# Shared transposes of q and k, a negated maximum, a spare buffer for the solve, and a longer search for the order

## The chip, the cores and the metric

The kernel runs on one core of one Trainium2 chip. The time is device microseconds (us) of one execution; several runs are taken and the median is the figure. A lower time is better.

## The reference

One layer of an encoder with two head groups, on x of 2048 rows and 1024 columns. After an RMSNorm, one projection gives the inputs of both groups:

- the delta-rule group: 4 heads of width 128, a centred convolution of 5 taps and SiLU on q, k and v, then a gated delta rule that is scanned forward and backward, a gated RMSNorm and a SiLU gate;
- the attention group: 8 query heads and 2 key heads of width 64, blocks of 128 queries that see three blocks of keys.

```
q = rotary(rms_norm(q, q_norm_w), cos, sin)
k = rotary(rms_norm(k, k_norm_w), cos, sin)
scores = einsum('bnqhgd,bnkhd->bnhgqk', qb, kb) * (SWA_HEAD_DIM ** -0.5)
scores = where(valid, scores, -inf)
mx = maximum(max(scores, axis=-1, keepdims=True), sink)
p = exp(scores - mx)
denom = sum(p, axis=-1, keepdims=True) + exp(sink - mx)
out = einsum('bnhgqk,bnkhd->bnqhgd', p / denom, vb)
...
m = where(strict, einsum('bhncd,bhnsd->bhncs', k_beta, k) * decay, 0.0)
t_inv = triangular_solve(eye + m, eye, left_side=True, lower=True, unit_diagonal=True)
...
x = x + concatenate([dn, sw]) @ w_out
```

## The kernel before

Matrix products of the projections keep two float32r halves of each operand, a rounded value (`hi`) and the rest (`lo`), and add three products.

**First part** (`phase_a`). `seq_chunk` projects 16 chunks of 128 rows to the attention's q, k and v and stores them in HBM; `gate_pairs` (tiles `pf_z`) and `conv_pair` (tiles `pf_c`, DVE line 241) project the gates and the convolution's inputs. For every chunk, `kv_chunk` and `q_chunk` load their rows and call `rope`: GpSimd (POOL) multiplies with the rotary table (lines 276 to 279), ScalarE (ACT) squares (281), VectorE (DVE) sums (282), POOL takes the power (283, 284), and DVE scales the rows (285). Then the result is split into hi and lo in SBUF (lines 303 and 304 for k, 321 and 322 for q). Each pair of hi and lo is transposed by TensorE (PE) as one 128x128 block: four transposes for a chunk of k (308), four for each of a chunk's two groups of q (326). One ACT copy takes them from PSUM (309, 327). `attend` computes the scores of a chunk in two groups of four heads (343, 344), adds the mask and takes the maximum with the sink as its start (345, DVE), negates the maximum (349), exponentiates (350, ACT), forms the denominator (353 to 357), scales p on POOL (359), transposes p (364), splits it (368, 369) and multiplies with v (371, 372).

**Second part** (`phase_b`). For each of the four delta heads in turn: `pre_front` (transposes, products `gh` at 695, DVE line 704, and line 709, which stores the matrices `m_d` to HBM), `solve`, `invert`, `scan`. `solve` inverts the diagonal 32x32 blocks of all chunks at once: two loads (732 into X, 733 into L), a transposing copy X to L (735), two fills of X on POOL (736, 737), then 31 steps of two DVE instructions (742, 746), and a store (747). `invert` loads these blocks (758), transposes them on DVE (759), puts them into the diagonals of `e1`, `e2` and `e3` by 12 POOL copies (764, 766, 768) for each of four groups `hi`, and multiplies (773, tiles `pi`). `scan` walks 16 steps forward and backward. While head h is scanned, the front, solve and inversion of head h+1 and the output projection of the attention rows (`sw_units`, tiles `pcs`) stand between its steps. The end is the output projection of the delta rows (`out_half`, tiles `pcd`).

**The order.** `set_order` fixes one instruction queue per engine before the program is built. It models the duration of each instruction, plans the whole program backward and forward 12 times, and keeps the plan with the earliest modelled end. The list `started` holds pairs of instructions whose starts must keep the program's order without the second waiting for the first's end.

Of the kernel before, what the change touches and what calls it, by code (L numbers as in the profile page):

```python
# [7 lines left out]
F32 = mybir.dt.float32  # L8
F32R = mybir.dt.float32r
# [6 lines left out]
P = 128  # L16
# [51 lines left out]
def phase_a(ctx, wide, tc, t, ident, nw, bd, gp, mix_sw, kq_d, v_d, zdn_d, zsw_d, q_pool):  # L68
# [24 lines left out]
    for a, src in ((qw, t["qw"]), (kw, t["kw"])):  # L93
        dma(a[:, 0], src.partition_broadcast(P))
        dma(a[:, 1, 0:32], src[32:64].partition_broadcast(P))
        dma(a[:, 1, 32:64], src[0:32].partition_broadcast(P))
    sink = const("sink", [P, NQ], t["sinks"].partition_broadcast(P))
    edge = const("edge", [P, 12, 4])
    half_neg = const("half_neg", [P, 16])
    V.memset(half_neg, -0.5)  # L100
    A.activation(cw, cw, AF.Copy, scale=0.5)
    A.activation(qw, qw, AF.Copy, scale=0.125)

    xhi, xlo = {}, {}

# [166 lines left out]
    def rope(src, n, tab, name):  # L272
        sv = src.rearrange("p (h d) -> p h d", d=64)
        t1 = sp.tile([P, 8, 64], F32, tag="t1", name=f"t1{name}")[:, :n]
        t2 = sp.tile([P, 8, 64], F32, tag="t2", name=f"t2{name}")[:, :n]
        G.tensor_tensor(t1, sv, tab[:, 0:1].to_broadcast([P, n, 64]), ALU.mult)
# [7 lines left out]
        G.tensor_tensor(rs, rs, half_neg[:, :n], ALU.pow)  # L284
        V.tensor_tensor(t1, t1, rs.unsqueeze(2).to_broadcast([P, n, 64]), ALU.mult)
        return t1

    def kv_chunk(c):
        sl = c % 4 + 2
        if c and c % 4 == 0:  # L290
            V.tensor_copy(k2[:, :, :, 0 : 2 * P], k2[:, :, :, 4 * P : 6 * P].bitcast(F32))
            V.tensor_copy(v2[:, 0:2], v2[:, 4:6].bitcast(F32))
        kv = sp.tile([P, 2 * P], F32, tag="kv", name=f"kv{c}")
        dma(kv, kv_d[c])
        kk = kv[:, 0:P]
        vv = kv[:, P : 2 * P].rearrange("p (h d) -> p h d", d=64)
        A.activation(v2[:, sl, :, 0:64], vv, AF.Copy)
        G.tensor_tensor(v2[:, sl, :, 64:128], vv, v2[:, sl, :, 0:64].bitcast(F32), ALU.subtract)
        kn = rope(kk, 2, rope_tab(c, kw, "k"), f"k{c}")
        kd = sp.tile([P, 512], F32R, tag="qd", name=f"kd{c}")  # L300
        kd = kd.rearrange("p (g s a d) -> p g s a d", g=2, s=2, a=2)
        knb = kn.unsqueeze(2).to_broadcast([P, 2, 2, 64])
        A.activation(kd[:, :, 0], knb, AF.Copy)
        V.tensor_tensor(kd[:, :, 1], knb, kd[:, :, 0].bitcast(F32), ALU.subtract)
        pt = pst.tile([P, 4, P], F32, tag="pst", name=f"ptk{c}")
        for g in range(2):
            for s in range(2):
                T.transpose(pt[:, 2 * g + s], kd[:, g, s].rearrange("p a d -> p (a d)").bitcast(F32), ident)
        A.activation(k2[:, :, :, sl * P : (sl + 1) * P], pt.rearrange("p (g s) n -> p g s n", g=2), AF.Copy)

    def q_chunk(c):
        qq = sp.tile([P, 512], F32, tag="qq", name=f"ql{c}")
        dma(qq, q_d[c])
        tab = rope_tab(c, qw, "q")
        r = []
        qa = rope(qq, 8, tab, f"q{c}")
        for g in range(2):
            qn = qa[:, 4 * g : 4 * g + 4]
            qd = sp.tile([P, 512], F32R, tag="qd", name=f"qd{c}_{g}")
            qd = qd.rearrange("p (h a d) -> p h a d", h=4, a=2)  # L320
            A.activation(qd[:, :, 0], qn, AF.Copy)
            V.tensor_tensor(qd[:, :, 1], qn, qd[:, :, 0].bitcast(F32), ALU.subtract)
            q2 = sp.tile([P, 4, P], F32R, tag="q2", name=f"q2_{c}_{g}", bufs=4)
            pt = pst.tile([P, 4, P], F32, tag="pst", name=f"ptq{c}_{g}")
            for j in range(4):
                T.transpose(pt[:, j], qd[:, j].rearrange("p a d -> p (a d)").bitcast(F32), ident)
            A.activation(q2, pt, AF.Copy)
            r.append(q2)
        return r

    def attend(c, q2):
# [3 lines left out]
        k0 = (sl - 1 + lo) * P  # L335
        for g in range(2):
            pr = [sp.tile([P, 3 * P], F32, tag="pr", name=f"pr{c}_{g}_{j}", bufs=6) for j in range(4)]
            st = sp.tile([P, 4, 4], F32, tag="st", name=f"st{c}_{g}")
            mx, nm, den, es = (st[:, i] for i in range(4))
            for j in range(4):  # L340
                hh = 4 * g + j
                ps = pss.tile([P, 3 * P], F32, tag="pss", name=f"s{c}_{hh}")
                T.matmul(ps[:, :n], q2[g][:, j], k2[:, g, 0, k0 : k0 + n], start=True, stop=False)
                T.matmul(ps[:, :n], q2[g][:, j], k2[:, g, 1, k0 : k0 + n], start=False, stop=True)
                V.tensor_tensor_reduce(  # L345
                    pr[j][:, :n], ps[:, :n], mask[:, lo * P : hi * P], 1.0, sink[:, hh : hh + 1],
                    ALU.add, ALU.max, accum_out=mx[:, j : j + 1],
                )
                V.tensor_scalar(nm[:, j : j + 1], mx[:, j : j + 1], -1.0, None, ALU.mult)  # L349
                A.activation(  # L350
                    pr[j][:, :n], pr[j][:, :n], AF.Exp, bias=nm[:, j : j + 1], accum_out=den[:, j : j + 1]
                )
            V.tensor_tensor(es, sink[:, 4 * g : 4 * g + 4], mx, ALU.subtract)
            A.activation(es, es, AF.Exp)
            V.scalar_tensor_tensor(den, den, 1.0, es, ALU.mult, ALU.add)
            V.tensor_scalar(den, den, 2.0, None, ALU.mult)
            V.reciprocal(den, den)  # L357
            for j in range(4):
                G.tensor_scalar(pr[j][:, :n], pr[j][:, :n], den[:, j : j + 1], 1.0, ALU.mult, ALU.mult)  # L359
# [161 lines left out]
def phase_b(ctx, wide, late, tc, t, ident, consts, hp, mix_dn, mix_sw, kq_d, v_d, zdn_d, zsw_d, dp, out):  # L521
# [204 lines left out]
    def solve(h, H):  # L726
        m_d, x_d, _ = H["solve"]
        L = qa.tile([P, 32, 32], F32, tag="L", name=f"L{h}")
        X = qa.tile([P, 32, 32], F32, tag="X", name=f"X{h}")
        lv = [m_d[d].rearrange("u (p y) -> (u p) y", p=4)[:, : 32 * P] for d in range(2)]  # L730
        lv = [a.rearrange("q (r x) -> q r x", x=P)[:, :, :32] for a in lv]
        dma(X[0:64], lv[0])
        dma(L[64:128], lv[1])
        x = X.rearrange("p r c -> p (r c)")
        V.tensor_copy(L[0:64], X[0:64].rearrange("p r c -> p c r"))
        G.memset(x, 0.0)
        G.memset(x[:, ::33], 1.0)
        for c in range(31):
            n = 31 - c
            tm = qa.tile([P, 256], F32, tag="tm", name=f"tm{h}_{c}")  # L740
            tv = tm[:, : n * (c + 1)].rearrange("p (r k) -> p r k", k=c + 1)
            V.tensor_tensor(
                tv, L[:, c + 1 :, c : c + 1].to_broadcast([P, n, c + 1]),
                X[:, c : c + 1, 0 : c + 1].to_broadcast([P, n, c + 1]), ALU.mult,
            )
            V.tensor_tensor(X[:, c + 1 :, 0 : c + 1], X[:, c + 1 :, 0 : c + 1], tv, ALU.subtract)
        dma(x_d.rearrange("d u (p r) c -> (d u p) (r c)", p=4), X.rearrange("p r c -> p (r c)"))

    def invert(h, H):
        _, x_d, mp = H["solve"]  # L750
        for hi in range(4):
# [8 lines left out]
                x0[d], x1[d] = (xc, xt) if d == 0 else (xt, xc)  # L760
            g = qb.tile([P, 4, P], F32, tag="g", name=f"g{h}_{hi}", bufs=2)
            G.tensor_tensor(g, m[:, :, 0], m[:, :, 1], ALU.add)
            for p, q in enumerate(quads):
                G.tensor_copy(e1[q, :, q], x0[p % 2][q])
            for p, q in enumerate(quads):
                G.tensor_copy(e2[q, :, q], x1[1 - p % 2][q])
            for p, q in enumerate(quads):
                G.tensor_copy(e3[q, :, q], x0[p // 2][q])

            def prod(j, lhs, rhs):  # L770
                o = ps_i[(hi + j) % 2].tile([P, 4, P], F32, tag="inv", name=f"pi{j}_{h}_{hi}")
# [167 lines left out]
def set_order(tc):  # L939
# [61 lines left out]
    for k, (i, eng) in enumerate(insts):  # L1001
        touched = [(a, False) for a in aps(i.ins)] + [(a, True) for a in aps(i.outs)]
        for a, w in touched:
# [14 lines left out]
            if psum and eng != "PE" and past and past[-1][1] != "PE" and past[-1][0] != k:  # L1018
                if past[-1][1] == eng:
                    started[past[-1][0]].append(k)  # L1020
                else:
                    edge(past[-1][0], k)
            past.append((k, eng, w, b))

    home, stacks, spans, gone, behind = {}, {}, {}, [], {}
# [213 lines left out]
    for i in range(12):  # L1239
# [3 lines left out]
        now = plan([-(b + d) for b, d in zip(back[1], dur)], True)  # L1243
        if i >= 7 and (best is None or now[0] < best[0]):
            best = now
    end, begin, queue = best
    info = mybir.DependencyInfo(mybir.DependencyClass.NoSync, mybir.DependencyReason.DATA)
    for e in ENGINES:
# [5 lines left out]
def layout(inputs):  # L1254
# [22 lines left out]
    cs = np.ascontiguousarray(cs.reshape(NCH, P, 2, 64).transpose(1, 0, 2, 3))  # L1277
    i, j = np.arange(P)[:, None], np.arange(P)[None, :]
    rel = np.arange(3 * P)[None, :] - P - i
    smask = np.where(np.abs(rel) <= 128, f(0), f(NEG)).astype(f)  # L1280
    le = (i <= j)
    tri = np.stack([le, ~le | (i == j), np.ones((P, P), bool)], 1).astype(f)
    dmask = np.stack([np.where(le, f(0), f(NEG)), np.where(i >= j, f(0), f(NEG))], 1).astype(f)
# [26 lines left out]
```

## Time and profile before

| | |
|---|---|
| median of 3 runs | 1288.86 us (1288.18 to 1288.86) |
| the profiled execution | 1286.12 us |
| its span in the trace | 1284.2 us |
| PE busy | 1227.4 us, 96% |
| DVE busy | 901.8 us, 70% |
| ACT busy | 718.8 us, 56% |
| POOL busy | 507.8 us, 40% |
| bytes moved by DMA | 205.35 MB, mean 160 GB/s |

Matmuls are pipelined and their ends are modelled: two of them may overlap in the record, and a busy PE is not PE at its peak. PEld is the load of weights, which runs beside the matmuls. The names of lines (L326) are lines of the kernel before.

### The profile page before, as it was taken

The numbers are of one execution on the slowest core, as the hardware profiler recorded it, in microseconds if no ns is written. First come the engines' busy times: TensorE is split into PE (matmuls) and PEld (weight loads), VectorE is DVE, ScalarE is ACT, GpSimd is POOL, SyncE is SP. The second block draws the span as 40 slices with busy tenths as digits, with TensorE's granted clock in tenths as the row PEclk, the third lists the DMA queues.
The fourth block names the chain that finished last, engine by engine and source line by source line (L and its number), as shares of the span: only waits on it lengthen the run. The fifth ranks groups of instructions, "written<-read, shape, count | busy, mean of one in ns | idle before, by whom it ended". The sixth has DMA issues, their size and how long they took to land.

```text
span 1284.2 us, 22568 instructions
## 1 busy us (share of the span) xinstructions
PE 1227.4 (96%) x7162; PEld 1056.0 (82%) x7162; DVE 901.8 (70%) x2266; ACT 718.8 (56%) x2121; POOL 507.8 (40%) x876
## 2 busy tenths in 40 slices
PE   6999999999999999999999998899799899999998
PEld 6998878788889987888888787788688789898776
DVE  4422488999874679999996583689489779557333
ACT  6421265776644677777665425858557855666210
POOL 2230054566512387774321306513681651641000
PEclk9999999999999999999999999999899999999999
DMA  7442254223544333421237816967965874746765
GB/s 259 150 127 79 97 169 158 88 83 101 177 130 131 121 106 111 124 98 50 75 115 242 237 63 196 283 192 206 278 172 157 242 202 139 207 148 201 242 233 210
DMA packets 225510, 205.35 MB, mean 160 GB/s; under 512 B 48496, under 2 KB 175088, under 8 KB 225392
## 3 DMA queue, kind: packets, MB, share of 16 engines
q1 hardware_dynamic: 225392, 203.92, 51.2%
q8 instruction: 57, 0.93, 0.3%
q14 instruction: 61, 0.50, 0.1%
HBM read 138.79 MB, written 65.08 MB: 159 GB/s over the span
## 4 chain that ended last, share of the span: by engine, by line
PE 67%; DVE 9%; DMA 9%; ACT 5%; POOL 4%; issue 4%; SPq 1%; DVEq 0%; POOLq 0%; ACTq 0%
PE pf_c L190 5%; PE pf_c L191 5%; PE pf_c L192 5%; PE pf_z L190 4%; PE pf_z L191 4%; PE pf_z L192 4%; PE pi L773 3%; PE pt L364 3%; PE pcd L562 2%; PE pcd L563 2%; PE pcd L564 2%; DVE acc L241 2%; PE pcs L601 2%; PE py L822 1%; PE pcs L600 1%
## 5 line engine op out<-in xcount | busy, mean ns | idle before, releaser
L190 PE MATMUL pf_c<-xhi,wh_c 128*128 128x512 f32 x384 | 151.3, 405 | 1.1 <-DVE acc L241 1.1
L191 PE MATMUL pf_c<-xlo,wh_c 128*128 128x512 f32 x384 | 152.0, 404 | 0.0
L192 PE MATMUL pf_c<-xhi,wl_c 128*128 128x512 f32 x384 | 150.6, 404 | 0.0
L241 DVE SCALAR_TENSOR_TENSOR acc<-pf_c,cw,acc 128x512 f32<-128x512 f32 (+1 forms) x192 | 140.4, 742 | 10.4 <-ACT acc L237 8.1
L359 POOL TENSOR_SCALAR pr<-pr,st 128x384 f32<-128x384 f32 (+1 forms) x128 | 88.8, 711 | 72.3 <-DVE st L357 56.5
L190 PE MATMUL pf_z<-xhi,wh_z 128*128 128x512 f32 x256 | 87.0, 403 | 0.5 <-DVE zo L214 0.5
L191 PE MATMUL pf_z<-xlo,wh_z 128*128 128x512 f32 x256 | 86.5, 399 | 0.0
L350 ACT ACTIVATE pr<-pr,st 128x384 f32<-128x384 f32 (+1 forms) x128 | 76.1, 597 | 17.7 <-DVE st L349 16.4
L192 PE MATMUL pf_z<-xhi,wl_z 128*128 128x512 f32 x256 | 85.3, 398 | 0.0
L190 PEld LDWEIGHTS pf_c<-xhi,wh_c 128*128 128x128 f32 x384 | 72.5, 189 | 14.8 <-DVE acc L241 1.5
L192 PEld LDWEIGHTS pf_c<-xhi,wl_c 128*128 128x128 f32 x384 | 72.2, 189 | 13.2
L191 PEld LDWEIGHTS pf_c<-xlo,wh_c 128*128 128x128 f32 x384 | 72.1, 189 | 13.1
L368 ACT ACTIVATE ph<-pt 128x512 fp32r<-128x512 f32 x92 | 53.8, 595 | 41.6 <-PE pt L364 38.2
L345 DVE CUSTOM_DVE_ANT_0 pr<-s,mask,sink 128x384 f32<-128x384 f32 (+1 forms) x128 | 73.0, 592 | 5.7 <-PE pt L364 3.2
L364 PE MATMUL pt<-ident,pr 128*128 128x128 f32 x368 | 72.1, 275 | 3.7 <-DVE pl L369 2.3
L369 DVE TENSOR_TENSOR pl<-pt,ph 128x512 fp32r<-128x512 f32 x92 | 62.0, 682 | 15.7 <-ACT ph L368 14.1
L827 ACT ACTIVATE yk<-py,ck 128x128 f32<-128x128 f32 x120 | 43.9, 366 | 44.6 <-PE py L822 43.3
L364 PEld LDWEIGHTS pt<-ident,pr 128*128 128x128 f32 x368 | 48.0, 140 | 20.2 <-DVE pl L369 4.3
L704 DVE SCALAR_TENSOR_TENSOR ma<-gh,bp,dc 128x256 f32<-128x256 f32 x128 | 54.6, 475 | 11.4 <-PE gh L695 7.6
L600 PE MATMUL pcs<-wohs,mhs 128*128 128x512 f32 x128 | 57.7, 451 | 5.0 <-ACT mhs L594 5.0
L201 PE MATMUL pq_q<-wh_q,xhi 128*128 128x256 f32 x256 | 60.6, 286 | 0.1
L202 PE MATMUL pq_q<-wh_q,xlo 128*128 128x256 f32 x256 | 60.0, 282 | 0.0
(253 smaller groups left out, 3743.7 us busy)
## 6 DMA issues: line engine op xcount, KB each, us to landing
kqc<-kq_d SPq DMA_DIRECT2D x120, 128.0 KB, 2.9
ws_c<-wt SPq DMA_DIRECT2D x48, 256.0 KB, 3.2
xr<-x SPq DMA_DIRECT2D x16, 512.0 KB, 5.5
ws_z<-wt SPq DMA_DIRECT2D x32, 256.0 KB, 3.7
kq<-kq_d SPq DMA_DIRECT2D x16, 512.0 KB, 5.1
m_d<-ma SPq DMA_DIRECT2D x32, 256.0 KB, 5.9
mxs<-mix_sw SPq DMA_DIRECT2D x32, 256.0 KB, 3.3
xrs<-x SPq DMA_DIRECT2D x32, 256.0 KB, 3.5
```

The lines of the kernel that those rows point to most:

```text
L190: T.matmul(ps, hi[:, k, cs], xhi[b][:, k], start=(k == 0), stop=False)
L191: T.matmul(ps, hi[:, k, cs], xlo[b][:, k], start=False, stop=False)
L192: T.matmul(ps, lo[:, k, cs], xhi[b][:, k], start=False, stop=(k == KC - 1))
L201: T.matmul(ps[:, :n], xh, hi[:, k, :n], start=(k == 0), stop=False)
L202: T.matmul(ps[:, :n], xl, hi[:, k, :n], start=False, stop=False)
L241: V.scalar_tensor_tensor(av, ps[:, lo:], cw[:, i, k : k + 1], av, ALU.mult, ALU.add)
L345: V.tensor_tensor_reduce(pr[j][:, :n], ps[:, :n], mask[:, lo * P : hi * P], 1.0, sink[:, hh : hh + 1], ALU.add, ALU.max, accum_out=mx[:, j ...
L350: A.activation(pr[j][:, :n], pr[j][:, :n], AF.Exp, bias=nm[:, j : j + 1], accum_out=den[:, j : j + 1])
L359: G.tensor_scalar(pr[j][:, :n], pr[j][:, :n], den[:, j : j + 1], 1.0, ALU.mult, ALU.mult)
L364: T.transpose(pt[:, j], pr[j][:, (kb - lo) * P : (kb - lo + 1) * P], ident)
L369: V.tensor_tensor(pl, ptf, ph.bitcast(F32), ALU.subtract)
L600: T.matmul(ps, mh[:, k], wh[:, k], start=(k == 0), stop=False)
```

## The change

1. The rows of q are no longer split before the transposes. Two heads of 64 columns stand beside each other in one 128x128 transpose; two transposes instead of four for each group. From PSUM, ACT copies hi and DVE subtracts to get lo, 64 partitions at a time. The row scaling of q moves from DVE to POOL. For k, DVE's row scaling writes each head twice beside itself, two transposes replace four, and ACT and DVE split what is in PSUM.
2. The weight of q, the sink and the mask get a negative sign, so that the maximum becomes a minimum that is the exponential's bias as it is; the negation (line 349) goes. A factor of 2 goes from the denominator (356) into POOL's scaling (359).
3. `solve` loads one half into a buffer of the ring `kq` instead of into X; the two fills of X stand ahead of the copy to L.
4. `invert` spreads the 12 copies of its first group (`hi` 0) over DVE, POOL and ACT; the three other groups stay on POOL.
5. `set_order` makes matmuls into one PSUM tile start in the program's order, and plans 120 further times, every fourth time from the best plan with random shifts of up to 1000 modelled nanoseconds.

```diff
     sink = const("sink", [P, NQ], t["sinks"].partition_broadcast(P))
+    G.tensor_scalar(sink, sink, -1.0, None, ALU.mult)
...
-    A.activation(qw, qw, AF.Copy, scale=0.125)
+    A.activation(qw, qw, AF.Copy, scale=-0.125)
...
-        V.tensor_tensor(t1, t1, rs.unsqueeze(2).to_broadcast([P, n, 64]), ALU.mult)
+        if n == 2:
+            kd = sp.tile([P, 2, 2, 64], F32, tag="kd", name=f"kd{name}")
+            rb = rs.unsqueeze(2).unsqueeze(3).to_broadcast([P, 2, 2, 64])
+            V.tensor_tensor(kd, t1.unsqueeze(2).to_broadcast([P, 2, 2, 64]), rb, ALU.mult)
+            return kd
+        G.tensor_tensor(t1, t1, rs.unsqueeze(2).to_broadcast([P, n, 64]), ALU.mult)
         return t1
...
         kn = rope(kk, 2, rope_tab(c, kw, "k"), f"k{c}")
-        kd = sp.tile([P, 512], F32R, tag="qd", name=f"kd{c}")
-        kd = kd.rearrange("p (g s a d) -> p g s a d", g=2, s=2, a=2)
-        knb = kn.unsqueeze(2).to_broadcast([P, 2, 2, 64])
-        A.activation(kd[:, :, 0], knb, AF.Copy)
-        V.tensor_tensor(kd[:, :, 1], knb, kd[:, :, 0].bitcast(F32), ALU.subtract)
-        pt = pst.tile([P, 4, P], F32, tag="pst", name=f"ptk{c}")
+        pt = pst.tile([P, 4, P], F32, tag="pst", name=f"ptk{c}")[:, :2]
         for g in range(2):
-            for s in range(2):
-                T.transpose(pt[:, 2 * g + s], kd[:, g, s].rearrange("p a d -> p (a d)").bitcast(F32), ident)
-        A.activation(k2[:, :, :, sl * P : (sl + 1) * P], pt.rearrange("p (g s) n -> p g s n", g=2), AF.Copy)
+            T.transpose(pt[:, g], kn[:, g].rearrange("p a d -> p (a d)"), ident)
+        kc = slice(sl * P, (sl + 1) * P)
+        A.activation(k2[:, :, 0, kc], pt, AF.Copy)
+        V.tensor_tensor(k2[:, :, 1, kc], pt, k2[:, :, 0, kc].bitcast(F32), ALU.subtract)
...
-            qd = sp.tile([P, 512], F32R, tag="qd", name=f"qd{c}_{g}")
-            qd = qd.rearrange("p (h a d) -> p h a d", h=4, a=2)
-            A.activation(qd[:, :, 0], qn, AF.Copy)
-            V.tensor_tensor(qd[:, :, 1], qn, qd[:, :, 0].bitcast(F32), ALU.subtract)
             q2 = sp.tile([P, 4, P], F32R, tag="q2", name=f"q2_{c}_{g}", bufs=4)
-            pt = pst.tile([P, 4, P], F32, tag="pst", name=f"ptq{c}_{g}")
-            for j in range(4):
-                T.transpose(pt[:, j], qd[:, j].rearrange("p a d -> p (a d)").bitcast(F32), ident)
-            A.activation(q2, pt, AF.Copy)
+            pt = pst.tile([P, 4, P], F32, tag="pst", name=f"ptq{c}_{g}")[:, :2]
+            for j in range(2):
+                T.transpose(pt[:, j], qn[:, 2 * j : 2 * j + 2].rearrange("p h d -> p (h d)"), ident)
+            for j in range(2):
+                A.activation(q2[0:64, j::2], pt[64 * j : 64 * j + 64], AF.Copy)
+                V.tensor_tensor(q2[64:128, j::2], pt[64 * j : 64 * j + 64], q2[0:64, j::2].bitcast(F32), ALU.subtract)
...
-                    ALU.add, ALU.max, accum_out=mx[:, j : j + 1],
+                    ALU.add, ALU.min, accum_out=nm[:, j : j + 1],
                 )
-                V.tensor_scalar(nm[:, j : j + 1], mx[:, j : j + 1], -1.0, None, ALU.mult)
                 A.activation(
-                    pr[j][:, :n], pr[j][:, :n], AF.Exp, bias=nm[:, j : j + 1], accum_out=den[:, j : j + 1]
+                    pr[j][:, :n], pr[j][:, :n], AF.Exp, bias=nm[:, j : j + 1], scale=-1.0, accum_out=den[:, j : j + 1]
                 )
...
-            V.scalar_tensor_tensor(den, den, 1.0, es, ALU.mult, ALU.add)
-            V.tensor_scalar(den, den, 2.0, None, ALU.mult)
+            V.tensor_tensor(den, den, es, ALU.add)
             V.reciprocal(den, den)
             for j in range(4):
-                G.tensor_scalar(pr[j][:, :n], pr[j][:, :n], den[:, j : j + 1], 1.0, ALU.mult, ALU.mult)
+                G.tensor_scalar(pr[j][:, :n], pr[j][:, :n], den[:, j : j + 1], 0.5, ALU.mult, ALU.mult)
...
-        dma(X[0:64], lv[0])
+        lt = q1.tile([P, 2, 512], F32, tag="kq", name=f"lt{h}", bufs=2).rearrange("p a s -> p (a s)")
+        lt = lt.rearrange("p (r c) -> p r c", c=32)
+        dma(lt[0:64], lv[0])
         dma(L[64:128], lv[1])
         x = X.rearrange("p r c -> p (r c)")
-        V.tensor_copy(L[0:64], X[0:64].rearrange("p r c -> p c r"))
         G.memset(x, 0.0)
         G.memset(x[:, ::33], 1.0)
+        V.tensor_copy(L[0:64], lt[0:64].rearrange("p r c -> p c r"))
...
-            for p, q in enumerate(quads):
-                G.tensor_copy(e1[q, :, q], x0[p % 2][q])
-            for p, q in enumerate(quads):
-                G.tensor_copy(e2[q, :, q], x1[1 - p % 2][q])
-            for p, q in enumerate(quads):
-                G.tensor_copy(e3[q, :, q], x0[p // 2][q])
+            for s, a, b in zip("GGG" if hi else "VGA", (e1, e2, e3), ([0, 1, 0, 1], [1, 0, 1, 0], [0, 0, 1, 1])):
+                xs = x1 if a is e2 else x0
+                for q, k in zip(quads, b):
+                    if s == "A":
+                        A.activation(a[q, :, q], xs[k][q], AF.Copy)
+                    else:
+                        (V if s == "V" else G).tensor_copy(a[q, :, q], xs[k][q])
...
+            if psum and eng == "PE":
+                mate = next((p for p in reversed(past) if p[1] == "PE"), None)
+                if mate and mate[0] != k:
+                    started[mate[0]].append(k)
...
+    for i in range(120):
+        width = (0, 1000)[i % 4 == 0]
+        start = best if i % 4 == 0 else now
+        back = plan([-(b + d) + noise(width) for b, d in zip(start[1], dur)], False)
+        now = plan([-(b + d) for b, d in zip(back[1], dur)], True)
+        if now[0] < best[0]:
+            best = now
...
-    smask = np.where(np.abs(rel) <= 128, f(0), f(NEG)).astype(f)
+    smask = np.where(np.abs(rel) <= 128, f(0), f(-NEG)).astype(f)
```

More of the change, by code (lines that the diff above doesn't have):

```diff
@@ L337, in attend @@
             pr = [sp.tile([P, 3 * P], F32, tag="pr", name=f"pr{c}_{g}_{j}", bufs=6) for j in range(4)]
-            st = sp.tile([P, 4, 4], F32, tag="st", name=f"st{c}_{g}")
-            mx, nm, den, es = (st[:, i] for i in range(4))
+            st = sp.tile([P, 3, 4], F32, tag="st", name=f"st{c}_{g}")
+            nm, den, es = (st[:, i] for i in range(3))
             for j in range(4):
@@ L346, in attend @@
                     pr[j][:, :n], ps[:, :n], mask[:, lo * P : hi * P], 1.0, sink[:, hh : hh + 1],
-                    ALU.add, ALU.max, accum_out=mx[:, j : j + 1],
+                    ALU.add, ALU.min, accum_out=nm[:, j : j + 1],
                 )
-                V.tensor_scalar(nm[:, j : j + 1], mx[:, j : j + 1], -1.0, None, ALU.mult)
                 A.activation(
-                    pr[j][:, :n], pr[j][:, :n], AF.Exp, bias=nm[:, j : j + 1], accum_out=den[:, j : j + 1]
+                    pr[j][:, :n], pr[j][:, :n], AF.Exp, bias=nm[:, j : j + 1], scale=-1.0, accum_out=den[:, j : j + 1]
                 )
-            V.tensor_tensor(es, sink[:, 4 * g : 4 * g + 4], mx, ALU.subtract)
+            V.tensor_tensor(es, nm, sink[:, 4 * g : 4 * g + 4], ALU.subtract)
             A.activation(es, es, AF.Exp)
-            V.scalar_tensor_tensor(den, den, 1.0, es, ALU.mult, ALU.add)
-            V.tensor_scalar(den, den, 2.0, None, ALU.mult)
+            V.tensor_tensor(den, den, es, ALU.add)
             V.reciprocal(den, den)
             for j in range(4):
-                G.tensor_scalar(pr[j][:, :n], pr[j][:, :n], den[:, j : j + 1], 1.0, ALU.mult, ALU.mult)
+                G.tensor_scalar(pr[j][:, :n], pr[j][:, :n], den[:, j : j + 1], 0.5, ALU.mult, ALU.mult)
             po = pso.tile([P, 512], F32, tag="pso", name=f"po{c}_{g}")
@@ L1245, in set_order, with noise @@
             best = now
+    seed = 1
+    def noise(width):
+        nonlocal seed
+        seed = (seed * 1103515245 + 12345) % 2**31
+        return width * (seed / 2**30 - 1)
+    for i in range(120):
[5 more added lines that the diff above has]
+            best = now
     end, begin, queue = best
```

## The prediction

> **What bounds the kernel now.** I read the busy line of the page first, then the windows by stage (columns: length, then busy time of PE, PEld, DVE, ACT, POOL with counts, the granted clock, DMA share, GB/s), then the waits of PE in the first part (total, times, longest).
>
> ```profile
> PE 1227.4 (96%) x7162; PEld 1056.0 (82%) x7162; DVE 901.8 (70%) x2266; ACT 718.8 (56%) x2121; POOL 507.8 (40%) x876
> ```
>
> ```profile
> 0.00:50.00 50.00, 38.43 (x262) 36.55 (x263) 25.34 (x41) 29.14 (x61) 14.71 (x36) 0.97 0.70 242
> 50.00:450.00 400.00, 396.35 (x2279) 343.18 (x2279) 265.15 (x598) 202.12 (x451) 152.20 (x242) 1.00 0.38 120
> 450.00:520.00 70.00, 68.41 (x402) 58.52 (x402) 61.08 (x158) 50.84 (x133) 57.36 (x78) 1.00 0.37 109
> 520.00:680.00 160.00, 158.28 (x809) 129.82 (x808) 154.53 (x382) 111.20 (x269) 74.50 (x108) 1.00 0.28 93
> 680.00:760.00 80.00, 79.53 (x367) 64.59 (x366) 51.58 (x116) 34.30 (x114) 16.08 (x18) 1.00 0.67 199
> 760.00:1060.00 300.00, 271.53 (x1770) 238.18 (x1768) 221.73 (x651) 197.81 (x777) 146.38 (x296) 0.98 0.72 209
> 1060.00:1284.20 224.20, 214.88 (x1285) 185.13 (x1284) 122.38 (x326) 93.41 (x317) 46.59 (x100) 0.99 0.61 197
> ```
>
> ```profile
> PE pt L364 <- DVE pl L369: 2.3, 4, 0.9
> PE pt L364 <- POOL pr L359: 1.3, 3, 0.7
> ```
>
> From 50 to 680 us, the stage of the attention and the convolution, PE is busy 396.35 + 68.41 + 158.28 = 623.0 of 630 us: TensorE is the bound, and whatever leaves its queue there comes off the time, unless another engine is right behind it. DVE is: 154.53 of 160 us from 520 on. In the stage of the scans, 760 to 1060, PE is idle for 300 - 271.5 = 28.5 us; there latency between engines costs as well. The two waits show how little PE waits for others in the first part: the longest totals are 2.3 and 1.3 us.
>
> The profiled execution took 1286.12 us for a span of 1284.2, so 1.9 us lie around the span; it is 2.7 us (0.2%) under the median of 1288.86 us. The sum below is a difference worked out in the profiled execution, taken off the median.
>
> **Transposes.** What one transpose costs PE's queue is read from starts, since the modelled ends overlap. First the timeline of PE (start, duration), then the group of line 326 (busy, mean ns, idle before):
>
> ```profile
> 283.18 0.40 PE L191 MATMUL pf_c<-xlo,wh_c 128*128 128x512 f32 x1
> 283.41 0.60 PE L308 MATMUL ptk<-ident,kd 128*128 128x128 f32 x4
> 283.77 0.48 PE L192 MATMUL pf_c<-xhi,wl_c 128*128 128x512 f32 x1
> 284.09 0.39 PE L190 MATMUL pf_c<-xhi,wh_c 128*128 128x512 f32 x1
> ```
>
> ```profile
> L326 PE MATMUL ptq<-ident,qd 128*128 128x128 f32 x128 | 20.5, 272 | 0.0
> ```
>
> A convolution matmul steps by 283.41 - 283.18 = 0.23 us. From 283.41 to 284.09 the queue passed four transposes and one such matmul: (0.68 - 0.23) / 4 = 0.1125 us each. The edit removes 64 of 128 transposes of q and, by the code, 32 of 64 of k: 96 x 0.1125 = **10.8 us**. By busy time it would be 20.5 / 128 x 96 = 15.4 us, which counts the last overlap of each group; I take the starts. They belong to the chunks of the attention, so nearly all lie in the stage where PE has no slack.
>
> The Trainium skill ("TensorE: Matmul & The Clock Gate", Part 4: PE-mode transpose) gives about 275 ns for a transpose inside a kernel. The mean of 272 ns agrees as a duration; as a price in a filled queue, 96 x 0.275 = 26.4 us (an estimate from that page), the step between starts speaks against it.
>
> **The splits of q and k, the maximum.** DVE loses lines 285 (for q), 349 and 322 and gains 64 subtractions from PSUM on 64 partitions; ACT loses 321 and 327 and gains 64 copies. The nearest rows for the new forms are 378 and 375, which read 64 partitions of PSUM with 256 elements each:
>
> ```profile
> L285 DVE TENSOR_TENSOR t1q<-t1q,rsq 128x512 f32<-128x512 f32 x16 | 16.2, 1015 | 5.9 <-POOL rsq L284 3.7 <-POOL acc L231 2.1
> L349 DVE TENSOR_SCALAR st<-st 128x1 f32<-128x1 f32 x128 | 16.1, 144 | 0.2
> ...
> L322 DVE TENSOR_TENSOR qd<-t1q,qd 128x256 fp32r<-128x256 f32 x32 | 15.0, 476 | 0.6 <-ACT qd L321 0.5
> ...
> L378 DVE TENSOR_TENSOR ot<-po,ot 64x256 f32<-64x256 f32 x32 | 13.4, 418 | 0.9
> ```
>
> ```profile
> L327 ACT ACTIVATE q<-ptq 128x512 fp32r<-128x512 f32 x32 | 18.7, 594 | 4.7 <-PE ptq L326 4.2
> ...
> L321 ACT ACTIVATE qd<-t1q 128x256 fp32r<-128x256 f32 x32 | 12.9, 414 | 7.6 <-DVE t1q L285 4.4 <-PE ptk L308 2.7
> ...
> L375 ACT ACTIVATE ot<-po 64x256 f32<-64x256 f32 x32 | 12.2, 381 | 26.2 <-PE po L372 25.9
> ```
>
> DVE: -16.2 - 16.1 - 15.0 + 64 x 0.418 = **-20.5 us**. ACT: -18.7 - 12.9 + 64 x 0.381 = **-7.2 us**. For k both change by less, with one DVE instruction replacing one in each of two places. These engines are not the bound, so I cost this at nothing; but it is what lets DVE follow when PE gets shorter, so the 10.8 us are not stopped by DVE's 97% from 520 on.
>
> POOL takes the row scaling of q, 16 instructions. Its price is that of POOL's nearest one, the other 128x512 multiplication with a broadcast operand; beside it, what a DVE instruction with two inputs in SBUF (line 304: min/median/max ns) does at worst:
>
> ```profile
> L276 POOL TENSOR_TENSOR t1q<-ql,tabq 128x512 f32<-128x512 f32 x16 | 21.5, 1342 | 39.9 <-DMA ql<-q_d 23.3 <-DVE qd L322 11.0 <-DVE st L353 4.8
> ```
>
> ```profile
> L304 DVE TENSOR_TENSOR kd<-t1k,kd x16: 407/416/1425, 37.3 to 606.1; 128x256 fp32r<-128x256 f32 x16
> ```
>
> 16 x 1.342 = **21.5 us** more on POOL. Its cover is the chunk of lead: `q_chunk` of a chunk stands ahead of `attend` of the one before it. I cost it at 0; if the cover is gone, at up to 21.5 us (a rival below). A gain on PE from it is excluded, since no PE instruction goes with it.
>
> **Solve.** The fills of X now wait for no copy. DVE and POOL in the first solve:
>
> ```profile
> 735.73 1.12 DVE L735 COPY L<-X 64x1024 f32<-64x1024 f32 x1 [0.63 <-DMA X<-m_d]
> 738.11 0.21 DVE L742 TENSOR_TENSOR tm<-L,X 128x31 f32<-128x31 f32 x1 [1.26 <-POOL X L737]
> ```
>
> ```profile
> 736.90 0.95 POOL L736 MEMSET X<- 128x1024 f32 x1 [2.79 <-DVE L L735]
> 737.92 0.16 POOL L737 MEMSET X<- 128x32 f32 x1
> ```
>
> The first step starts 738.11 - 736.85 = 1.26 us after the copy, all of it the fills and their handing over. That goes in each of four solves. In the first, PE has the gates' matmuls to do (79.53 of 80 us), so nothing is won; for heads 1 to 3 the solve stands ahead of the scan in a stage in which PE idles: 3 x 1.26 = **3.8 us**, between 0 (other work covers it) and 3.8. The load moves to another buffer with the same bytes and the same queue; it holds one of two `kq` buffers until the copy, and the next front's second load waits behind that, which I cost at 0 since the next front starts after the solve's copy.
>
> **Diagonal blocks.** The first inversion's 12 copies go from one engine to three:
>
> ```profile
> 917.94 1.16 PE L773 MATMUL pi<-iv,g 128*128 128x128 f32 x8 [0.22 <-POOL iv L764]
> ```
>
> PE waited 0.22 us for them here. Three heads at 0 to 0.22 us: I take 0.
>
> **The search.** It changes the order of nearly everything by a little and promises nothing by itself. Reading the two programs' PE queues side by side, the units come in nearly the same succession, with a front of head 1 now ahead of the first inversion as the largest move; so neither a gain nor a loss can be read from the order. What it can touch is idle time and what follows from it, the clock. The four stretches with a lowered clock:
>
> ```profile
> 28.00:36.00 8.00, 7.84 (x52) 7.72 (x52) 1.89 (x4) 5.25 (x11) 4.05 (x11) 0.79 1.03 382
> 800.00:804.00 4.00, 2.88 (x14) 2.88 (x15) 2.19 (x6) 1.88 (x10) 1.38 (x4) 0.60 0.81 175
> 908.00:920.00 12.00, 9.14 (x33) 6.74 (x34) 5.19 (x13) 4.44 (x15) 6.12 (x11) 0.72 0.95 276
> 1112.00:1120.00 8.00, 6.77 (x36) 5.96 (x36) 3.60 (x8) 5.67 (x18) 7.14 (x17) 0.79 0.47 127
> ```
>
> The last three lost 0.40 x 4 + 0.28 x 12 + 0.21 x 8 = 6.6 us. An order with fewer gaps may lose none of it, one with more may lose as much again: -6.6 to +6.6, and I take 0.
>
> **Sum:** 1288.86 - 10.8 - 3.8 = **1274.3 us**. Its own range goes from 1274.3 - 4.6 (transposes at busy time) - 6.6 = 1263 to 1288.86 - 10.8 + 6.6 = 1285.
>
> **The rivals.**
> *Held PSUM buffers, no change.* A group of q now holds its PSUM buffer for two copies and two subtractions, 2 x 0.381 + 2 x 0.418 = 1.6 us, instead of one copy of 0.594: 1.0 us more for 32 groups, 32 us over two buffers that the transposes of p (364) use too, so 16 us if PE lost all of it: 1290. It decides from 14.6 us of stalls. For it: PE waited for DVE's freeing of them (2.3 us). Against: that is all there was in 630 us.
> *POOL becomes the bound, slower.* If the 21.5 us all fall on the path to the scores and to p's scaling (359): 1274.3 + 21.5 = 1296; over 14.6 us of it the kernel is slower. For it: 57.36 of 70 us busy from 450 on, and line 304 stretched from 416 to 1425 ns, so the two engines do hold each other up. Against: 74.50 of 160 us from 520 on, and DVE's instructions with two SBUF inputs get fewer. The Trainium skill ("SBUF — State Buffer", SBUF: two separate sides) calls the port pair of VectorE and GpSimd an exclusive lock for a whole instruction; the stretched row agrees, and by that rule the price would fall on DVE too.
> *Half of the scans' idle time goes.* The search removes 14.2 of 28.5 us: 1260. Against: the two queues have nearly the same succession of units.
> *Each transpose is worth its whole 272 ns:* 96 x 0.272 = 26.1, so 1288.86 - 26.1 - 3.8 = 1259. Against: the starts. This is what the page on TensorE would make of it.
>
> **How the numbers follow.** Forecast 0.67, held buffers 0.07, POOL 0.10, idle time 0.13, whole durations 0.03. A measurement can tell 0.2% (2.6 us) from no change. Faster is 0.67 + 0.13 + 0.03 = 0.83, the same 0.07, slower 0.10. The range is that of the forecast, reached down to 1260 for the idle time: 1260 to 1285 leaves out 0.07 + 0.10 + 0.03 = 0.20.
>
> **What would show it.** Right: 96 fewer transposes on PE with the same step; 50 to 680 us shortened by about 11 us with PE still above 98%; DVE about 20 us less; the first solve step right behind the copy. Wrong: line 364 waiting for many us on DVE or POOL, POOL near full from 450 to 520, more than 28.5 us of idle PE in the scans, or more stretches with a lowered clock.

## The result

The changed kernel takes 1281.38 us (median of 6 runs, 1277.77 to 1285.56) against 1288.86 us before (6 runs, 1287.14 to 1294.34): a ratio of 0.994, 95% interval 0.9921 to 0.9959, so 7.7 us less (5.3 to 10.2). The forecast was 14.6 us less. The time lies in the range, and the way is right, but the experiments show that the reason was not: the gain comes from the step that I had put at nothing, and the step that I had put at 10.8 us brought almost none of it. That the time came to lie in the range is luck. The profiled execution has a span of 1279.7 us, 4.5 us less than before.

The busy line of the changed kernel's page, then its windows by stage (the columns of the windows before):

```profile
PE 1220.6 (95%) x7066; PEld 1043.9 (82%) x7066; DVE 902.3 (71%) x2138; ACT 714.2 (56%) x2121; POOL 501.2 (39%) x861
```

```profile
50.00:450.00 400.00, 392.88 (x2194) 333.36 (x2193) 262.73 (x519) 194.46 (x432) 150.26 (x248) 1.00 0.37 118
450.00:520.00 70.00, 69.22 (x410) 58.69 (x409) 59.52 (x141) 49.54 (x138) 60.72 (x86) 1.00 0.37 113
520.00:680.00 160.00, 156.94 (x776) 127.02 (x775) 153.72 (x332) 109.57 (x270) 74.08 (x112) 0.99 0.29 95
680.00:760.00 80.00, 79.78 (x367) 64.62 (x366) 43.67 (x96) 34.87 (x114) 14.52 (x16) 1.00 0.67 194
760.00:1060.00 300.00, 269.78 (x1765) 237.61 (x1764) 232.42 (x682) 200.58 (x786) 138.63 (x272) 0.98 0.73 210
```

PE has 96 instructions fewer (7162 to 7066). From 50 to 680 us it is busy 619.0 us where it was 623.0, and DVE 476.0 us where it was 480.8: DVE did not get 20 us lighter. What the transposes freed is not time gained. The last row of the convolution's matmuls (min/median/max ns, first to last start), before and after:

```profile
L192 PE MATMUL pf_c<-xhi,wl_c x384: 387/394/508, 129.6 to 681.8; 128*128 128x512 f32 x192
```

```profile
L193 PE MATMUL pf_c<-xhi,wl_c x384: 387/394/776, 128.1 to 683.7; 128*128 128x512 f32 x192
```

The first part ends 1.9 us later than before, at 683.7 instead of 681.8 us, in these two executions, so their 4.5 us lie behind it: 596.0 us are left there instead of 602.4. One execution of each places them only roughly. Five of the kernels below have the changed kernel's queues, and what lies behind the first part is the same in them; it took 594.7 to 600.1 us.

### The profile page after: what moved, and what is told of

Read it like the earlier page. It is cut to its first block, busy times and chain, and to the rows that moved or that the text cites. A ratio compares the mean times of both kernels' runs of the same rounds, so it can differ in the third digit from the quotient of the medians.

```text
span 1279.7 us, 22162 instructions
## 1 busy us (share of the span) xinstructions
PE 1220.6 (95%) x7066; PEld 1043.9 (82%) x7066; DVE 902.3 (71%) x2138; ACT 714.2 (56%) x2121; POOL 501.2 (39%) x861
## 4 chain that ended last, share of the span: by engine, by line
PE 68%; DVE 10%; DMA 8%; issue 5%; ACT 5%; POOL 3%; SPq 1%; POOLq 0%; DVEq 0%; ACTq 0%
PE pf_c L191 5%; PE pf_c L192 5%; PE pf_c L193 5%; PE pf_z L191 4%; PE pf_z L193 4%; PE pf_z L192 4%; PE pi L774 3%; PE pt L362 3%; PE pq_q L202 2%; PE pq_q L203 2%; PE pq_q L204 2%; DVE acc L242 2%; PE pcs L598 2%; PE po L832 1%; PE py L823 1%
## 5 line engine op out<-in xcount | busy, mean ns | idle before, releaser
L191 PE MATMUL pf_c<-xhi,wh_c 128*128 128x512 f32 x384 | 154.8, 408 | 1.1 <-DVE acc L242 1.1
L193 PE MATMUL pf_c<-xhi,wl_c 128*128 128x512 f32 x384 | 151.9, 403 | 0.0
L242 DVE SCALAR_TENSOR_TENSOR acc<-pf_c,cw,acc 128x512 f32<-128x512 f32 (+2 forms) x192 | 141.4, 744 | 12.8 <-ACT acc L238 10.7
L357 POOL TENSOR_SCALAR pr<-pr,st 128x384 f32<-128x384 f32 (+1 forms) x128 | 80.7, 650 | 98.2 <-DVE st L355 63.8
L191 PE MATMUL pf_z<-xhi,wh_z 128*128 128x512 f32 x256 | 98.8, 403 | 0.1
L192 PE MATMUL pf_z<-xlo,wh_z 128*128 128x512 f32 x256 | 98.2, 402 | 0.0
L193 PE MATMUL pf_z<-xhi,wl_z 128*128 128x512 f32 x256 | 97.1, 401 | 0.0
L193 PEld LDWEIGHTS pf_c<-xhi,wl_c 128*128 128x128 f32 x384 | 72.5, 189 | 13.4
L345 DVE CUSTOM_DVE_ANT_0 pr<-s,mask,sink 128x384 f32<-128x384 f32 (+1 forms) x128 | 73.7, 595 | 10.8 <-PE s L344 8.2
L366 ACT ACTIVATE ph<-pt 128x512 fp32r<-128x512 f32 x92 | 53.9, 596 | 47.0 <-PE pt L362 35.1
L202 PE MATMUL pq_q<-wh_q,xhi 128*128 128x256 f32 x256 | 67.8, 289 | 0.3 <-ACT sgkv L261 0.3
L204 PE MATMUL pq_q<-wl_q,xhi 128*128 128x256 f32 x256 | 67.9, 285 | 0.0
L203 PE MATMUL pq_q<-wh_q,xlo 128*128 128x256 f32 x256 | 67.7, 285 | 0.0
```

Source lines behind the costliest of these rows:

```text
L191: T.matmul(ps, hi[:, k, cs], xhi[b][:, k], start=(k == 0), stop=False)
L192: T.matmul(ps, hi[:, k, cs], xlo[b][:, k], start=False, stop=False)
L193: T.matmul(ps, lo[:, k, cs], xhi[b][:, k], start=False, stop=(k == KC - 1))
L202: T.matmul(ps[:, :n], xh, hi[:, k, :n], start=(k == 0), stop=False)
L203: T.matmul(ps[:, :n], xl, hi[:, k, :n], start=False, stop=False)
L204: T.matmul(ps[:, :n], xh, lo[:, k, :n], start=False, stop=(k == KC - 1))
```

## The experiments

All ratios are to the kernel before on the same chip, five rounds each; "first part" is the last start of the row above in the one profiled execution. The experiments ran on three chips, and the changed kernel was not run again beside them: a difference "by the ratios" takes its ratio of 0.994 to hold on each of them.

**The edits without the search, and the search without the edits.** The first takes lines out of `set_order` of the changed kernel, the second puts the same lines into the kernel before:

```diff
-            if psum and eng == "PE":
-                mate = next((p for p in reversed(past) if p[1] == "PE"), None)
-                if mate and mate[0] != k:
-                    started[mate[0]].append(k)
...
-    for i in range(120):
...
```

> The changed kernel with the order planned as before: no 120 further plans and no rule for matmuls into one PSUM tile. Theory A (the new order gave part of the transposes' gain back by idle time, alternation of tiles and lowered clock in the first part): 1274 to 1279 us, faster than the changed kernel's 1281. Theory B (the search helped, and the transposes brought less than 10.8 us): 1283 to 1288 us. If any order is as good as another, within 2 us of 1281.

> The kernel before with the further search and the rule for matmuls into one PSUM tile alone. Theory A: 1290 to 1297 us, slower than before by what the order costs. Theory B: 1282 to 1286 us.

The edits with the old search: 1286.56 us, ratio 0.999 (0.998 to 1.0001), first part 686.6 us. The search alone: 1280.96 us, 0.9946 (0.993 to 0.9963), first part 680.1. Both went against theory A (the second came out 1 us under the range of theory B): the edits alone bring nothing that can be told, and the search alone brings all that the changed kernel has. "The search" means the 120 further plans and the rule for matmuls into one PSUM tile together; they were not tried one by one.

**The transposes put back, nothing else moved.** The changed kernel, with 96 more transposes into the free half of the same PSUM tile, each group right behind its pair in PE's queue; all queues are otherwise the same:

```diff
+            for j in range(2):
+                T.transpose(ptx[:, 2 + j], qn[:, 2 * j : 2 * j + 2].rearrange("p h d -> p (h d)"), ident)
```

> The changed kernel with 96 further transposes of the same rows into the unused half of the same PSUM tile, each right behind its pair, and every other instruction of every queue in the same place. The step read in the profile before (0.1125 us) gives 10.8 us more than the changed kernel, about 1292 us; whole durations of 0.272 us would give 26 us more, 1307; if the transposes hide in waits, 0 to 4 us more, 1281 to 1285.

1281.96 us, ratio 0.9948 (0.9933 to 0.9964): 1.0 us over the changed kernel by the ratios, give or take 3. The 10.8 us are excluded. It is not that a transpose is cheaper than I read. PE's timeline at the same place of the queue, in the changed kernel and then with the transposes back (line 331 holds the further pair):

```profile
283.10 0.39 PE L192 MATMUL pf_c<-xlo,wh_c 128*128 128x512 f32 x1
283.33 0.40 PE L193 MATMUL pf_c<-xhi,wl_c 128*128 128x512 f32 x1
283.69 0.41 PE L324 MATMUL ptq<-ident,t1q 128*128 128x128 f32 x2
283.85 0.48 PE L191 MATMUL pf_c<-xhi,wh_c 128*128 128x512 f32 x1
284.16 0.39 PE L192 MATMUL pf_c<-xlo,wh_c 128*128 128x512 f32 x1
```

```profile
283.64 0.39 PE L193 MATMUL pf_c<-xhi,wl_c 128*128 128x512 f32 x1
283.87 0.38 PE L329 MATMUL ptq<-ident,t1q 128*128 128x128 f32 x2
284.08 0.38 PE L331 MATMUL ptq<-ident,t1q 128*128 128x128 f32 x2
284.22 0.48 PE L191 MATMUL pf_c<-xhi,wh_c 128*128 128x512 f32 x1
284.54 0.39 PE L192 MATMUL pf_c<-xlo,wh_c 128*128 128x512 f32 x1
```

The step of a convolution matmul is still 0.23 us (283.10 to 283.33). From 283.87 to 284.54 the queue passed four transposes and one such matmul, (0.67 - 0.23) / 4 = 0.11 us each, as in the kernel before. But in the changed kernel the pair starts 0.36 us after the matmul ahead of it, not 0.23: there was a wait of 0.13 us, and no idle time is recorded, since that matmul's record lasts 0.40 us. With the further pair the wait is gone. From L193 to the second matmul behind the pair it is 0.83 us in the changed kernel and 0.90 with two more transposes: 0.07 us more instead of 0.22. So a wait of up to about 0.16 us behind a convolution matmul (record 0.39, step 0.23) leaves no trace in the busy share, and the busy share hid slack of this kind: with the transposes back the first part ended at 686.3 instead of 683.7 us, 2.6 us later for 10.8 us of added work, and PE's visible idle time from 50 to 680 us shrank only from 11.0 to 9.2 us, by the two kernels' windows (changed, then with the transposes back):

```profile
50.00:680.00 630.00, 619.03 (x3376) 519.07 (x3375) 475.97 (x992) 353.57 (x837) 285.06 (x445) 0.99 0.35 112
```

```profile
50.00:680.00 630.00, 620.84 (x3464) 527.85 (x3463) 472.68 (x990) 354.04 (x837) 285.24 (x445) 1.00 0.35 111
```

A part of the difference between these two executions may be the clock's: it was granted at 0.99 in the first window and at 1.00 in the second.

**What bounds the first part, then.** Four kernels keep the changed kernel's queues, written out, and change the length of instructions or add some behind their neighbours. The first cuts one of four convolution taps on DVE:

```diff
-                    av = acc[:, at + 2 - k + lo : at + 514 - k]
+                    hi = 512 if k < 4 else 64
+                    av = acc[:, at + 2 - k + lo : at + 2 - k + hi]
```

> The changed kernel, every instruction in the same place of its queue, with the last of the four convolution taps (48 DVE instructions of 0.74 us) cut to 64 of its 512 columns, so that part of the convolution is left out: about 26 us less for DVE in the first part. If DVE is as much the bound there as PE, PE's shorter queue now shows: 5 to 12 us under the changed kernel's 1281, 1269 to 1276. If PE alone is the bound: 1280 to 1282. If it is waits of another kind (POOL, the order itself): 1278 to 1281.

1274.72 us, 0.988 (0.9854 to 0.9907): 7.7 us under the changed kernel by the ratios, give or take 4; first part 676.9. DVE's busy time on the page falls by 22.5 us, from 902.3 to 879.8.

> The same with the 96 transposes back behind their pairs. If DVE hid the transposes, they now show: 8 to 11 us over the kernel with DVE relieved. If they hide in waits that DVE has no part in, 0 to 3 us over it.

1280.76 us, 0.9916 (0.9891 to 0.9941). The transposes now cost 4.6 us by the ratios instead of 1.0, with an uncertainty of about 4.6; between the two expectations. The last convolution row of the two kernels, without and with the transposes, puts the first part 1.5 us later, where it was 2.6 with DVE's whole work. So this pair does not show that DVE hid the transposes.

```profile
L192 PE MATMUL pf_c<-xhi,wl_c x384: 387/394/628, 129.3 to 676.9; 128*128 128x512 f32 x192
```

```profile
L192 PE MATMUL pf_c<-xhi,wl_c x384: 387/394/507, 128.4 to 678.4; 128*128 128x512 f32 x192
```

The third puts the negations back, as load without a reader:

```diff
+                V.tensor_scalar(st[:, 3, j : j + 1], nm[:, j : j + 1], -1.0, None, ALU.mult)
```

> The changed kernel with the 128 one-element negations back on DVE, each right behind its minimum, into a spare column that nobody reads; all else in the same place. By their durations (0.144 us) 18 us more work for DVE, by the step of 0.07 us that the timeline shows behind one of them 9 us. If DVE bounds the first part: 4 to 9 us over 1281, 1285 to 1290. If not: 0 to 2 us.

1292.19 us, 1.0006 (0.9985 to 1.0027): 8.5 us over the changed kernel by the ratios, give or take 4, near the top of what DVE as the bound would give. The first part is 10.9 us longer. Its last convolution row, its window, and PE's wait for the subtraction of q (2.8 us in total in the changed kernel):

```profile
L192 PE MATMUL pf_c<-xhi,wl_c x384: 387/394/775, 129.8 to 694.6; 128*128 128x512 f32 x192
```

```profile
50.00:680.00 630.00, 614.59 (x3339) 508.95 (x3338) 482.11 (x1105) 353.57 (x830) 283.62 (x441) 1.00 0.34 110
```

```profile
PE pt L363 <- DVE q L326: 3.9, 4, 2.7
```

PE is busy for 4.4 us less of this window than in the changed kernel and gets through 37 instructions less (3339, not 3376): it waits, and all that was added is on DVE. So 128 of DVE's smallest instructions cost 8.5 us where 96 transposes on PE cost 1.0; the uncertainties (4 and 3 us) leave the proportion open, not which of the two is more.

The fourth cuts POOL's work on q and p:

```diff
-        G.tensor_tensor(t1, t1, t2, ALU.add)
+        m = n if n == 2 else 1
+        G.tensor_tensor(t1[:, :m], t1[:, :m], t2[:, :m], ALU.add)
...
-                G.tensor_scalar(pr[j][:, :n], pr[j][:, :n], den[:, j : j + 1], 0.5, ALU.mult, ALU.mult)
+                G.tensor_scalar(pr[j][:, :64], pr[j][:, :64], den[:, j : j + 1], 0.5, ALU.mult, ALU.mult)
```

> The changed kernel, every instruction in the same place, with POOL's work on q (the addition and the row scaling) cut to 64 of 512 columns and its scaling of p to 64 of 384, so that part of the attention is left out: about 80 us less for POOL in the first part. If POOL, by its own time or by holding DVE up (one DVE subtraction took 4.13 us beside it), makes the waits: 4 to 10 us under 1281. If not: 1279 to 1282.

1275.42 us, 0.9875 (0.9847 to 0.9904): 8.4 us under the changed kernel by the ratios, give or take 4; first part 674.2. The busy line of its page:

```profile
PE 1216.8 (95%) x7066; PEld 1045.7 (82%) x7066; DVE 891.1 (70%) x2138; ACT 712.5 (56%) x2121; POOL 433.8 (34%) x861
```

POOL is busy for 67.4 us less, not 80. POOL's work counts in the first part, though POOL is busy for 45% of it (285.06 of 630 us). DVE is busy for 11.2 us less as well (902.3 to 891.1) with the same instructions, so a part of POOL's price is paid on DVE; how large a part, this run does not tell. One way is seen in the changed kernel; DVE, POOL and PE around 536 us, then two matmuls of PE in what follows:

```profile
535.19 0.62 DVE L345 CUSTOM_DVE_ANT_0 pr<-s,mask,sink 128x384 f32<-128x384 f32 x1
535.74 0.08 DVE L345 DVE_READ_ACCUMULATOR2_ANT st<- 128x1 f32 x1
535.74 4.13 DVE L183 TENSOR_TENSOR wl_c<-ws_c,wh_c 128x512 fp32r<-128x512 f32 x1
```

```profile
534.85 1.30 POOL L280 TENSOR_TENSOR t1q<-t1q,t2q 128x512 f32<-128x512 f32 x1
536.10 0.33 POOL L279 TENSOR_TENSOR t2k<-kv,tabk 128x64 f32<-128x64 f32 x1
536.39 0.46 POOL L270 TENSOR_TENSOR tabq<-csq,qw 128x128 f32<-128x128 f32 x1
536.80 2.52 POOL L512 TENSOR_TENSOR gm<-gm,dmask 128x512 f32<-128x512 f32 x2
```

```profile
540.80 0.63 PE L362 MATMUL pt<-ident,pr 128*128 128x128 f32 x4 [2.49 <-DVE q L327]
...
542.85 0.63 PE L192 MATMUL pf_c<-xlo,wh_c 128*128 128x512 f32 x1
543.27 0.63 PE L193 MATMUL pf_c<-xhi,wl_c 128*128 128x512 f32 x1
```

A subtraction with two inputs in SBUF took 4.13 us; it ended at 539.87, 0.55 us after POOL's unbroken run (539.32). The subtraction of q (327) stood behind it and PE waited 2.49 us for that. The clock was 0.79 in the 8 us that followed; there a convolution matmul steps by 0.42 us (542.85 to 543.27). The Trainium skill ("SBUF — State Buffer", SBUF: two separate sides) has the two engines take the port pair for whole instructions; the record agrees, and here POOL's instructions followed each other without a gap in which DVE began.

**How much is the order.** Other starts of the random shifts, for the changed kernel and for the kernel before with the search alone:

```diff
-    seed = 1
+    seed = 2
```

> The changed kernel with another start of the random shifts, so another order of the same instructions. If the order decides by several us what the chip makes of the same work: 3 us or more away from 1281, either way (1270 to 1278, or 1284 to 1290). If not, within 2 us of it.

> The changed kernel with the third seed. If the edits bring something that orders can use: 1274 to 1279. If the order alone decides: anywhere from 1274 to 1287.

> The kernel before with the further search alone, random shifts of the second seed. With the first seed it took 1281, as much as the changed kernel. If the edits bring nothing by themselves and the second seed's order of the changed kernel (1275.6) was a lucky one: 1276 to 1286, with no link to the seed. If the edits bring 3 to 6 us once an order uses them: 1280 to 1283 here, so that the changed kernel's orders lie lower on average.

> The same with the third seed. The same two theories: 1276 to 1286 by chance alone, 1280 to 1283 if an order for the old instructions cannot go lower.

| seed | all edits and the search | the search alone |
|---|---|---|
| 1 | 0.994 (0.9921 to 0.9959) | 0.9946 (0.993 to 0.9963) |
| 2 | 0.9908 (0.9893 to 0.9924), 1275.55 us | 0.9929 (0.9912 to 0.9947), 1281.19 us |
| 3 | 0.9924 (0.9908 to 0.994), 1281.12 us | 0.9899 (0.9879 to 0.992), 1277.05 us |
| mean | 0.9924 | 0.9925 |

The means are equal: with three orders each, the edits bring nothing that shows, and the search brings 0.75%, 9.7 us. The seeds scatter so much that an effect of the edits of some 4 us either way would not show. The changed kernel's second seed lies 5.8 us under its first, the third at it, and the search alone reaches 1277.05 us with its third: the order decides, with no link to the seed's number. A seed moves the time by up to 0.5%. The best order found, the kernel before with the search and the third seed, beats the changed kernel by 0.4%, and its interval just does not touch the other's; it is the best of three.

What the search improves is not found. For the search alone, seeds 1 to 3, the spans are 1276.9, 1277.1 and 1278.1 us with PE busy for 1220.9, 1224.9 and 1223.3, so PE's visible idle time is 56.0, 52.2 and 54.8 us where it was 1284.2 - 1227.4 = 56.8. It explains 0.8, 4.6 and 2.0 of the 7.3, 7.1 and 6.1 us by which these spans are shorter. The first part ends at 680.1, 678.4 and 678.4 instead of 681.8 us, so 1.7, 3.4 and 3.4 us of the gain lie in it and 5.6, 3.7 and 2.7 behind it. The rest must lie in waits and steps that leave no idle time in the record; that is argued, not shown.

**A quarter of p's scaling on ACT**, with the second seed:

```diff
+                if j == 3:
+                    A.activation(pr[j][:, :n], pr[j][:, :n], AF.Copy, scale=den[:, j : j + 1])
+                else:
+                    G.tensor_scalar(pr[j][:, :n], pr[j][:, :n], den[:, j : j + 1], 1.0, ALU.mult, ALU.mult)
```

> The changed kernel with the second seed, and the scaling of p of every fourth head on ACT instead of POOL (32 instructions of about 0.65 us), with the factor of 2 back in the denominator (32 small DVE instructions, 2 us). POOL relieved of 80 us brought 8 us in the fixed order; a quarter of it may bring 2: 1271 to 1276 if DVE and POOL bound the first part, 1276 to 1282 if ACT is then late or the order is a worse one.

1280.34 us, 0.992 (0.9901 to 0.9938), against 0.9908 for the changed kernel with that seed: no gain. It got a new order as well, so this does not tell whether the scaling or the order took back what POOL's relief gave.

## Why the prediction was right in its range and wrong in its reasons

**What bounds the kernel.** Wrong. I took PE's 623.0 of 630 us for the bound. In the fixed order 10.8 us of work on PE cost 1.0 us, while about 9 us on DVE cost 8.5, and taking work from DVE or POOL brought 7.7 and 8.4 (3 us either way for PE, 4 for the others). I had named DVE as right behind at 97% from 520 us on, and then let the estimate of its relief answer it.

**Transposes, -10.8 us.** The price of one was right (0.11 us a step), the claim that all of it comes off the time was not: 1.0 us, with 3 either way.

**DVE, -20.5 us.** Mis-sized, and this is the term that should have stopped the step above. Its rows give durations, and DVE's instructions overlap. The timeline of before shows the step behind a negation, that of after the step behind a new subtraction:

```profile
539.83 0.14 DVE L349 TENSOR_SCALAR st<-st 128x1 f32<-128x1 f32 x1
539.90 0.67 DVE L369 TENSOR_TENSOR pl<-pt,ph 128x512 fp32r<-128x512 f32 x1
540.50 0.14 DVE L349 TENSOR_SCALAR st<-st 128x1 f32<-128x1 f32 x1
540.56 0.14 DVE L353 TENSOR_TENSOR st<-sink,st 128x4 f32<-128x4 f32 x1
```

```profile
534.74 0.42 DVE L327 TENSOR_TENSOR q<-ptq,q 64x256 fp32r<-64x256 f32 x1
535.19 0.62 DVE L345 CUSTOM_DVE_ANT_0 pr<-s,mask,sink 128x384 f32<-128x384 f32 x1
```

A negation takes 0.07 us of DVE's queue, not 0.144: 9.0 us in all, not 16.1. A subtraction on partitions 64 to 127 takes 0.45 us, more than its 0.42: 28.8 us, not 26.8. With lines 285 and 322 by their steps as well (15.2 us without idle time, and 10.9 us, the median step of 322 times its count), DVE loses 35.1 us and gains 28.8, net 6.3; the windows show 4.8 less. The Trainium skill ("VectorE: DVE Perf Modes", Two Vector instructions with no wait between them) says that an instruction whose input or output starts in another group of 32 partitions than the last one's is held until all earlier ones are done; a step longer than the duration fits that.

**POOL, +21.5 us at a cost of 0.** The size was near (the row below gives 18.2 us). The cost is unlikely to be nothing, since POOL's time counts in the first part: if all of POOL's work there is worth what the 67.4 us were, 18.2 us cost 18.2 / 67.4 x 8.4 = 2.3 us, an estimate. These 16 instructions were not tried by themselves.

```profile
L291 POOL TENSOR_TENSOR t1q<-t1q,rsq 128x512 f32<-128x512 f32 x16 | 18.2, 1136 | 0.4
```

**Solve, -3.8 us.** The wait for the fills went as I said, but bought nothing that can be told: the edits' mean is that of the search alone. In the kernel before, the second solve's first step starts 1.47 us after the copy's end (841.77 + 2.06 to 845.30). The second solve of the changed kernel:

```profile
844.82 1.21 DVE L737 COPY L<-lt 64x1024 f32<-64x1024 f32 x1 [1.05 <-DMA lt<-m_d]
845.96 0.33 DVE L835 SCALAR_TENSOR_TENSOR S<-S,egt,po 128x128 f32<-128x128 f32 x1
846.21 0.19 DVE L742 TENSOR_TENSOR tm<-L,X 128x31 f32<-128x31 f32 x1
```

Its first step starts 0.18 us after the copy's end. In the first solve it did not come right behind the copy (which ends at 746.58): the new order has DVE wait for ACT there first.

```profile
750.14 0.69 DVE L215 SCALAR_TENSOR_TENSOR zo<-zo,pf_z 128x512 f32<-128x512 f32 x1 [3.56 <-ACT zo L214]
...
751.94 0.20 DVE L742 TENSOR_TENSOR tm<-L,X 128x31 f32<-128x31 f32 x1
```

**Diagonal blocks, 0.** Too good: PE now waits for DVE's copies, 3.0 us at the longest, where it waited 0.22 for POOL's, as these waits of the changed kernel say. DVE's queue has the scan in it.

```profile
PE pi L774 <- DVE iv L769: 4.3, 2, 3.0
```

**The search, 0 of -6.6 to +6.6.** Wrong, and it is the whole gain: 9.7 us in the mean of three orders. I looked at the succession of units, which hardly changed, and so could not see smaller moves, which may be what counts. I bounded it by the clock alone, though my own rival had 28.5 us of idle time in the scans within its reach. That rival is not what happened either: PE's idle time from 760 to 1060 us is 30.2 us in the changed kernel, and with the search alone visible idle time in the whole kernel explains 2.5 of 6.8 us in the mean of three orders.

**The rivals.** POOL as a bound is right in part as a mechanism (less work on POOL shortened the first part, and a part of that came by way of DVE), not as a price of 21.5 us. Held PSUM buffers: the wait of line 364 (now 362) for DVE's q is 2.8 us, not 16. Whole durations of transposes: excluded by the steps of 0.11 us and by the transposes put back.

What stays open is which of the edits takes back what the removed negations and transposes give; the splits of q on 64 partitions, POOL's row scaling and DVE's diagonal copies are the candidates, and they were not run one by one. Another possibility was not tried either: what an instruction costs when it is added to a fixed order need not be what it costs in an order planned with it. The search alone plans for the negations and the 96 transposes and is as fast as the changed kernel.

## What to carry to other kernels

A busy share of 99% on PE does not make it the bound: where records of pipelined instructions are longer than their steps, short waits hide in them, so add work to one engine at a time in an unchanged order and see which one moves the time. Price instructions that overlap by the step between starts, not by their duration, on DVE as well as on PE. And where a planner rewrites the whole order, an edit is told from its order only by several orders of each: here the seed moved the time by up to 6 us, of the 7.7 us that the changed kernel gained. Work added to a fixed order is priced in that order alone; a planner that knows of it may place it where it costs less.

## What the hardware showed that I had not expected

- One DVE subtraction of 0.69 us took 4.13 us beside a run of POOL instructions.
- A DVE instruction that writes the upper 64 partitions held the next one for 0.45 us, longer than its own 0.42.
- A gap of 2.49 us on PE was followed by matmuls with a step of 0.42 instead of 0.23 us. The spread between the changed kernel's six runs goes with the clock: the slowest (1285.56 us) had a mean granted clock of 0.989, the fastest (1277.77) 0.994; 0.005 of 1280 us is 6.4 of the 7.8 us between them. In other kernels it does so less: the edits without the search took 1289.46 us at 0.993 and 1285.86 at 0.991.
